# Gated DeltaNet projections: convolution taps and SiLU traced later, decays a head ahead, last blocks reordered

## The chip, the cores and the metric

The kernel runs on one core of a Trainium2 chip. The metric is device time in microseconds of one execution. The engines named below are PE (TensorE), DVE (VectorE), ACT (ScalarE), POOL (GpSimd) and SP (SyncE, which here issues DMAs). Each takes its own instructions strictly in the order in which the compiled program holds them.

## The reference

A trunk of two layers over two groups of tokens, one of 1024 and one of 256, which the kernel handles as T = 1280 tokens. Layer 0 is a neighbourhood attention, layer 1 a bidirectional gated DeltaNet with 8 heads (keys of 128, values of 256, chunks of 64). The change is in layer 1:

```python
proj = h @ w_in
qkv = jax.nn.silu(_centred_depthwise_conv(proj[..., :o1], conv_w))   # 5 taps along the tokens
z = proj[..., o1:o2].reshape(b, t, GDN_HEADS, GDN_DV)
...
decay = jnp.where(tril, jnp.exp(jnp.where(tril, diff, 0.0)), 0.0)
a_kk = jnp.where(tril_strict, jnp.einsum('bhncd,bhnsd->bhncs', k_beta, k) * decay, 0.0)
lhs = jnp.eye(c, dtype=jnp.float32) + a_kk
w = lax.linalg.triangular_solve(lhs, k_beta * jnp.exp(g)[..., None], ...)
u = lax.linalg.triangular_solve(lhs, v * beta[..., None], ...)
...                                     # a scan over chunks, forward and backward
o = _rmsnorm(o, norm_w) * jax.nn.silu(z)
return o.reshape(b, t, GDN_VW) @ w_out
```

## The kernel before, in words

**Stages.** Layer 0 fills the first 750 us. `gdn_proj` (about 760 to 1600) makes everything that the scan of layer 1 needs: for each of 8 heads four blocks of 128 channels of q, k and v, and two blocks of z. Then `prep(..., alone=True)` prepares head 0, the scan of the heads runs (1633 to 2000), and the output projection ends the program.

**A block** is 128 channels times 1280 tokens, in three column pieces (512, 512, 256). For each piece PE runs 24 float matmuls (three products of high and low parts over eight slices of the width, line L1203) into a PSUM bank `mm`, which has three buffers. For q, k and v ACT copies the piece into a `raw` tile with borders for the convolution (L516). Then come the convolution's centre tap `acc` on ACT (L519), four further taps on DVE (L521, 128x1282 each), SiLU on ACT (`th`, L524), and a DMA to `qkv_spill` in DRAM (L525, L526). Channel `ch` of head `h` is 0 for q, 1 for k, 2 and 3 for v; the loop takes (0,1), then for each head 0, 2, 3 and the next head's 1. A z block takes tanh on ACT (L546) and a product on DVE (L549).

**The inversion.** As soon as a head's k is there, `invert` turns it into the inverse of the triangular matrices, all ten pairs of chunks at once:
- decays E: a matmul into a PSUM tile `t` (L584; `t` has three buffers), four additions on DVE (L587), Exp on ACT (L590), a DMA to `e_spill`, and the sum B of both directions on POOL (L604);
- pk = k.k on PE, also into `t` (L608), its diagonal (`junk`, L612) and B (L616) on DVE;
- D (L623), the transpose N (L632), X (L633), then **the sweep**: 30 steps of two DVE instructions, each depending on the last (L638, L640), and two transposes (L644, L645);
- copies of X on ACT (L653, L654) and of parts of W on POOL; then a wait of 34000 columns;
- four small groups of matmuls: L666, then Z on ACT (L669), L673, then DVE and ACT (L675 to L681), L686, Z (L689), L694, W (L696), and a DMA to `w_spill` (L697).

**What sets the order.** A `Side` object holds generators. While the block matmuls are traced, `side.tick(columns)` adds up their columns, and a generator whose due time is reached is traced up to its next `yield n`, after which it is due n columns later (times a pace). A block has 30,720 columns. The framework's scheduler then orders each engine's instructions from this trace; `keep_in_program_order` pins an instruction behind what was traced before it on its engine. In before, the taps and SiLU are traced at once after their block, and `invert` starts 26000 to 50000 columns behind its k block.

**The hand-over.** `factors` (L795 to L820) makes reciprocal square roots on DVE, with one small DMA. `prep` asks on SP for kT, qT, the decays Al, qe, vT and W (L840 to L859), all from DRAM, and its three groups of matmuls lead to the scan's first matmul (L967).

## Time and profile before

| | |
|---|---|
| median of 3 runs | 2265.09 us (2259.45 to 2268.21) |
| the profiled execution | 2260.98 us; span on the core 2259.2 us |
| mean granted clock of PE | 0.977 of full speed |
| DVE, ACT, POOL busy | 1509.4, 1127.4, 571.9 us |

The median lies 4 us above the profiled execution, whose durations are used throughout. A row of the profile has an engine, a line of the kernel, an operation and `out<-in` by tile names, then the shape and `xN` for N instructions; a number in square brackets is the idle time before it, with the engine and instruction that ended it. In a timeline the first number is the start in us from the span's start and the second the duration. PE's matmuls are pipelined: the distance between two starts is what one costs.

### The profile page before, as it was taken

What the parts mean: (1) busy time and instruction counts of PE and PEld (TensorE: products, weight loads), DVE (VectorE), ACT (ScalarE), POOL (GpSimd) and SP (SyncE); (2) the same over time, 40 slices, a digit from 0 to 9 for tenths busy, and PEclk for the clock granted to TensorE, in tenths of its full rate; (3) what the DMA queues carried; (4) which work ended last, traced back from release to release, by engine and by line L of the source; (5) the groups of instructions that cost most, each with busy time, mean ns of one, the idle gap of its engine ahead of it and who ended that gap; (6) DMA issues with size and microseconds to landing.
All of it is one profiled execution on the core that took longest, in us unless ns stands there. A gap on an engine that the chain in (4) does not pass through costs nothing.

```text
span 2259.2 us, 34060 instructions
## 1 busy us (share of the span) xinstructions
PE 2170.7 (96%) x12502; PEld 1885.4 (83%) x12502; DVE 1509.4 (67%) x3370; ACT 1127.4 (50%) x2299; POOL 571.9 (25%) x634
## 2 busy tenths in 40 slices
PE   8999999999989998999999999999799999999998
PEld 7789989989878877878888888888688888877887
DVE  5577777776763867858586776868466666676444
ACT  6455545555573454443444444454356666654233
POOL 2100100110231422212232222223176666600000
PEclk9999999999999998999999999999699999999999
DMA  5434343533555343535435353452575565567322
GB/s 180 111 74 117 81 117 74 124 93 99 154 156 170 97 114 103 148 93 133 135 101 162 91 146 100 145 143 78 182 206 166 167 186 179 149 217 234 109 96 85
DMA packets 148457, 300.10 MB, mean 133 GB/s; under 512 B 44977, under 2 KB 67633, under 8 KB 147265
## 3 DMA queue, kind: packets, MB, share of 16 engines
q1 hardware_dynamic: 126784, 232.89, 32.7%
q0 software_dynamic: 12096, 44.05, 11.1%
q10 hardware_dynamic: 9408, 20.98, 3.0%
q8 instruction: 99, 1.62, 0.3%
q14 instruction: 70, 0.57, 0.1%
HBM read 211.92 MB, written 75.45 MB: 127 GB/s over the span
## 4 chain that ended last, share of the span: by engine, by line
PE 36%; DVE 17%; ACT 4%; DMA 3%; issue 2%; POOL 1%; SPq 0%; DVEq 0%; ACTq 0%; POOLq 0%
PE mm L1203 17%; DVE acc L521 5%; DVE tmp L638 4%; DVE X L640 4%; PE k L967 3%; PE o L939 2%; PE u L939 2%; PE o L980 2%; PE k L958 2%; DMA e_spill<-E 1%; PE t L893 1%; PE m L1049 1%; DVE N L644 1%; PE m L673 1%; DMA yt<-y_spill 1%
## 5 line engine op out<-in xcount | busy, mean ns | idle before, releaser
L1203 PE MATMUL mm<-xh,wl 128*128 128x512 f32 (+1 forms) x1920 | 701.8, 366 | 3.9 <-DMA wl<-w_o 3.0
L1203 PE MATMUL mm<-xl,wh 128*128 128x512 f32 (+1 forms) x1920 | 702.7, 366 | 0.3 <-DVE xl L352 0.2
L1203 PE MATMUL mm<-xh,wh 128*128 128x512 f32 (+1 forms) x1920 | 701.3, 365 | 1.6 <-DVE t L189 0.7
L1203 PEld LDWEIGHTS mm<-xh,wl 128*128 128x128 f32 x1920 | 367.8, 192 | 47.2 <-DMA wl<-w_o 3.4
L1203 PEld LDWEIGHTS mm<-xh,wh 128*128 128x128 f32 x1920 | 367.9, 192 | 46.1 <-POOL xh L351 1.1
L1203 PEld LDWEIGHTS mm<-xl,wh 128*128 128x128 f32 x1920 | 367.5, 191 | 44.1 <-DVE xl L352 0.4
L521 DVE SCALAR_TENSOR_TENSOR acc<-raw,cw,acc 128x1282 f32<-128x1282 f32 x128 | 201.3, 1573 | 84.6 <-ACT acc L519 82.9
L1153 POOL CAST wh<-wraw 128x1024 fp32r<-128x1024 f32 x32 | 33.7, 1054 | 497.6 <-PE mm L1203 441.3
L1155 ACT ACTIVATE wh<-wraw 128x1024 fp32r<-128x1024 f32 x92 | 96.9, 1055 | 99.5 <-PE mm L1203 75.1
L1203 PE MATMUL mm<-yh,wh 128*128 128x512 f32 (+1 forms) x384 | 137.5, 359 | 2.4 <-ACT yh L1077 2.4
L1203 PE MATMUL mm<-yh,wl 128*128 128x512 f32 (+1 forms) x384 | 137.0, 358 | 1.2 <-DVE wl L1157 1.2
L1203 PE MATMUL mm<-yl,wh 128*128 128x512 f32 (+1 forms) x384 | 137.7, 360 | 0.3 <-DVE yl L1078 0.3
L971 DVE TENSOR_TENSOR vl<-k,vh 128x256 fp32r<-128x256 f32 x160 | 66.9, 422 | 69.9 <-ACT vh L970 65.4
L247 ACT ACTIVATE ph<-pt 128x512 fp32r<-128x512 f32 (+2 forms) x144 | 67.5, 478 | 76.0 <-PE pt L243 64.5
L248 DVE TENSOR_TENSOR pl<-pt,ph 128x512 fp32r<-128x512 f32 (+2 forms) x144 | 75.1, 538 | 37.7 <-ACT ph L247 36.1
L524 ACT ACTIVATE th<-acc 128x1282 f32<-128x1282 f32 x32 | 40.9, 1278 | 113.3 <-DVE acc L521 113.3
L1159 ACT ACTIVATE wl<-wraw 128x1024 fp32r<-128x1024 f32 x84 | 88.8, 1057 | 16.2 <-DMA wraw<-w_qk 8.1
L516 ACT ACTIVATE raw<-mm 128x512 f32<-128x512 f32 (+1 forms) x96 | 49.7, 521 | 94.2 <-PE mm L1203 93.0
L221 ACT ACTIVATE P<-P,mx 128x384 f32<-128x384 f32 (+1 forms) x128 | 75.0, 586 | 39.6 <-DVE mx L220 38.3
L1219 PE MATMUL mm<-wh,xl 128*128 128x256 f32 x320 | 92.4, 289 | 0.3 <-POOL xl L65 0.3
L1219 PE MATMUL mm<-wh,xh 128*128 128x256 f32 x320 | 92.3, 290 | 0.0
L1219 PE MATMUL mm<-wl,xh 128*128 128x256 f32 x320 | 92.1, 288 | 0.0
(315 smaller groups left out, 4871.8 us busy)
## 6 DMA issues: line engine op xcount, KB each, us to landing
wraw<-w_qkv SPq DMA_DIRECT2D x32, 512.0 KB, 3.9
qkv_spill<-th SPq DMA_DIRECT2D x32, 512.0 KB, 2.6
wraw<-w_go SPq DMA_DIRECT2D x32, 512.0 KB, 3.4
wl<-w_qkv POOLq DMA_DIRECT2D x30, 512.0 KB, 7.4
Al<-e_spill SPq DMA_DIRECT2D x8, 1280.0 KB, 6.8
qe<-eg_spill SPq DMA_DIRECT2D x16, 640.0 KB, 7.9
wraw<-w_qk SPq DMA_DIRECT2D x16, 512.0 KB, 4.0
wl<-w_qk POOLq DMA_DIRECT2D x16, 512.0 KB, 8.9
```

Of the source, the lines that this page charges most:

```text
L221: nc.scalar.activation(Pv, Pv, AF.Exp, scale=-1.0, bias=mx[:, 0:1], accum_out=mx[:, 1:2])
L247: nc.scalar.activation(view(ph), view(pt), AF.Copy)
L248: nc.vector.tensor_sub(view(pl), view(pt), view(ph))
L521: nc.vector.scalar_tensor_tensor(acc, r[:, i:i + m], cw[:, f, i:i + 1], acc, op0=OP.mult, op1=OP.add)
L638: nc.vector.tensor_mul(tv, N[:, 0:c, c:c + 1].to_broadcast([128, c, n]), X[:, c:c + 1, c + 1:32].to_broadcast([128, c, n]))
L640: nc.vector.tensor_add(X[:, 0:c, c + 1:32], X[:, 0:c, c + 1:32], tv)
L939: self.tc.nc.tensor.matmul(ps, w[x], v[y], start=(first and i == 0), stop=(i == 2))
L967: nc.tensor.matmul(pw, W[:, d, cs[d]], Y[d], start=True, stop=True)
L1155: nc.scalar.activation(wh, raw, AF.Copy)
L1159: nc.scalar.activation(wl, raw, AF.Copy, scale=-1.0)
L1203: nc.tensor.matmul(ps, w[:, k, :], x[k][b], start=(k == 0 and i == 0), stop=(k == KD - 1 and i == 2))
L1219: nc.tensor.matmul(ps, x[k][b][:, cc], w[:, k % 4, :], start=(k == 0 and i == 0), stop=(k == KD - 1 and i == 2))
```

## The change

- The taps and SiLU of a block become a generator `conv`. The taps are traced 8000 columns after the block and the first is pinned on DVE; SiLU is traced 14000 columns later for k and 20000 for the others, and pinned on ACT. `invert` is added from there, 4000 columns later.
- `raw` has two buffers in place of three, B two in place of one.
- The decays leave `invert` and become a generator `decays`. Head 0's follow the gates; head h+1's are added 4000 columns behind the sweep of head h. `invert` waits until they exist.
- `factors` moves from behind `gdn_proj` to the same point of head 7; its pool `cp` opens earlier.
- A z block's product and DMA become a generator `gated`, 3000 columns later, pinned on DVE.
- The last blocks: k of head 7 now comes ahead of the last v block of head 6. One z block follows head 7's k, and one the loop.
- In `prep`, when it runs alone, the vT loads come ahead of the others, the first two before Al.

Of the instructions only the table loads of ACT change in number, 34 to 48, and POOL's memsets by three.

```diff
@@ -466,11 +466,12 @@
         ap = st.enter_context(pool(tc, "gp", 2, "right"))
         pp = st.enter_context(banks(tc, "gpi", 2, "right"))
         side = a["side"] = Side()
-        side.add(gates(tc, a, ap, pmm, pp, XH, XL))
+        Bs = {}
+        side.add(chained(gates(tc, a, ap, pmm, pp, XH, XL), decays(tc, a, ap, pp, 0, Bs)))
         side.tick(0)
         cw = ap.tile([128, 32, 5], F32, name="cw", bufs=1)
         nc.sync.dma_start(cw, a["conv_w"])
-        raw = [ap.tile([128, T + 6], F32, name=f"raw{i}", bufs=1) for i in range(3)]
+        raw = [ap.tile([128, T + 6], F32, name=f"raw{i}", bufs=1) for i in range(2)]
         for r in raw:
             nc.gpsimd.memset(r[:, 0:2], 0.0)
             nc.gpsimd.memset(r[:, NP + 2:NP + 4], 0.0)
@@ -500,10 +501,32 @@
                 h, i = next(zs)
                 gate_z(tc, a, pmm, XH, XL, h, side, (i,))
 
-        for h, ch in [(0, 1)] + [(h + (ch == 1), ch) for h in range(8) for ch in (0, 2, 3, 1)][:-1]:
+        def conv(f, r):
+
+            h, ch = divmod(f, 4)
+            m = T + 2
+            acc = ap.tile([128, T + 2], F32, name="acc")
+            nc.scalar.activation(acc, r[:, 2:2 + m], AF.Copy, scale=cw[:, f, 2:3])
+            yield 8000
+            for i in (0, 1, 3, 4):
+                tap = nc.vector.scalar_tensor_tensor(acc, r[:, i:i + m], cw[:, f, i:i + 1], acc,
+                                                     op0=OP.mult, op1=OP.add)
+                if i == 0:
+                    tc.keep_in_program_order(tap)
+            yield 14000 if ch == 1 else 20000
+            th = ap.tile([128, T + 2], F32, name="th")
+            tc.keep_in_program_order(nc.scalar.activation(th, acc, AF.Silu))
+            nc.sync.dma_start(a["qkv_dram"][f, :, :NP], th[:, :NP])
+            nc.sync.dma_start(a["qkv_dram"][f, :, NP:], th[:, NP + 2:])
+            if ch == 1:
+                side.add(invert(tc, a, ap, pp, h, th, D, W, WT, Z, Bs), 4000, 0.85 if h == 7 else 0.95)
+
+        order = [(0, 1)] + [(h + (ch == 1), ch) for h in range(8) for ch in (0, 2, 3, 1)][:-1]
+        order[27:29] = order[28:26:-1]
+        for h, ch in order:
             f = 4 * h + ch
             wh, wl = a["first"].pop(0) if a["first"] else load_w(tc, a, a["w_qkv"][f])
-            r = raw[n_c % 3]
+            r = raw[n_c % 2]
             n_c += 1
             for b in sorted(range(3), key=lambda b: (f, b) not in a["begun"]):
                 t0, n = BLK[b]
@@ -514,23 +537,11 @@
                     proj(nc, ps, wh, wl, XH, XL, b, side)
                 o = 2 if t0 < NP else 4
                 nc.scalar.activation(r[:, t0 + o:t0 + o + n], ps, AF.Copy)
-            m = T + 2
-            acc = ap.tile([128, T + 2], F32, name="acc")
-            nc.scalar.activation(acc, r[:, 2:2 + m], AF.Copy, scale=cw[:, f, 2:3])
-            for i in (0, 1, 3, 4):
-                nc.vector.scalar_tensor_tensor(acc, r[:, i:i + m], cw[:, f, i:i + 1], acc,
-                                               op0=OP.mult, op1=OP.add)
-            th = ap.tile([128, T + 2], F32, name="th")
-            nc.scalar.activation(th, acc, AF.Silu)
-            nc.sync.dma_start(a["qkv_dram"][f, :, :NP], th[:, :NP])
-            nc.sync.dma_start(a["qkv_dram"][f, :, NP:], th[:, NP + 2:])
+            side.add(conv(f, r), 0)
+            side.tick(0)
             if ch == 1:
-                delay = {0: 32000, 1: 50000, 2: 37000}.get(h, 26000)
-                side.add(invert(tc, a, ap, pp, h, th, D, W, WT, Z), delay, 0.87 if h == 7 else 0.95)
-                if h != 1:
-                    gate_blocks(2 if h else 1)
-            elif (h, ch) == (1, 0):
-                gate_blocks(2)
+                gate_blocks(1 if h in (0, 7) else 2)
+        gate_blocks(1)
         side.drain()
 
 
@@ -538,6 +549,12 @@
 
     nc = tc.nc
     ws = [load_w(tc, a, a["w_z"][2 * h + i]) for i in halves]
+
+    def gated(u, z, ps, t0, n):
+        tc.keep_in_program_order(nc.vector.scalar_tensor_tensor(z, z, 1.0, ps, op0=OP.add, op1=OP.mult))
+        nc.sync.dma_start(a["z_dram"][u, :, t0:t0 + n], z)
+        yield 0
+
     for i, (wh, wl) in zip(halves, ws):
         for b, (t0, n) in enumerate(BLK):
             ps = pmm.tile([128, 512], F32, name="mm")[:, :n]
@@ -546,8 +563,12 @@
             tanh = nc.scalar.activation(z, ps, AF.Tanh, scale=0.5)
             if h == 7 and i:
                 tc.keep_in_program_order(tanh)
-            nc.vector.scalar_tensor_tensor(z, z, 1.0, ps, op0=OP.add, op1=OP.mult)
-            nc.sync.dma_start(a["z_dram"][2 * h + i, :, t0:t0 + n], z)
+            side.add(gated(2 * h + i, z, ps, t0, n), 3000)
+
+
+def chained(*gens):
+    for g in gens:
+        yield from g
 
 
 def alternate(*gens):
@@ -590,18 +611,30 @@
     nc.scalar.activation(E, E, AF.Exp)
 
 
-def invert(tc, a, ap, pp, h, kT, D, W, WT, Z):
+def decays(tc, a, ap, pp, h, Bs):
 
     nc = tc.nc
-    B = ap.tile([128, NB, 128], F32, name="B", bufs=1)
+    B = ap.tile([128, NB, 128], F32, name="B", bufs=2)
     for c0 in range(0, NB, 4):
         n = min(4, NB - c0)
         E = ap.tile([128, 2, 4, 128], F32, name="E", bufs=1)[:, :, :n]
         for d in range(2):
             decay(nc, a, ap, pp, h, d, c0, n, E[:, d], 3)
-            yield 2000
+            yield 3500
         nc.sync.dma_start(a["e_dram"][h, :, :, c0:c0 + n], E)
         nc.gpsimd.tensor_add(B[:, c0:c0 + n], E[:, 0], E[:, 1])
+    Bs[h] = B
+
+
+def invert(tc, a, ap, pp, h, kT, D, W, WT, Z, Bs):
+
+
+    nc = tc.nc
+    while h not in Bs:
+        yield 400
+    B = Bs.pop(h)
+    for c0 in range(0, NB, 4):
+        n = min(4, NB - c0)
         pk = pp.tile([128, 4, 128], F32, name="t", bufs=3)
         for c in range(n):
             k = kT[:, tok(c0 + c)]
@@ -660,6 +693,10 @@
         nc.gpsimd.tensor_copy(W[sl[i], 0, :, q], diag(i, 1 - lo))
         nc.gpsimd.tensor_copy(W[sl[i], 1, :, q], diag(i, lo))
         yield 0
+    if h < 7:
+        a["side"].add(decays(tc, a, ap, pp, h + 1, Bs), 4000)
+    else:
+        factors(tc, a)
     yield 34000
     zt = pp.tile([128, NB, 32], F32, name="m", bufs=2)
     for c in range(NB):
@@ -800,10 +837,10 @@
         nc.vector.scalar_tensor_tensor(y, t, 1.5, y, op0=OP.add, op1=OP.mult)
 
 
-def factors(tc, a, cp):
+def factors(tc, a):
 
     nc = tc.nc
-    ss = a["ss"]
+    ss, cp = a["ss"], a["cp"]
     nw = cp.tile([128, 2], F32, name="nw")
     nc.sync.dma_start(nw, a["norm_w"])
     nc.vector.tensor_scalar(nw, nw, 0.5, None, op0=OP.mult)
@@ -844,19 +881,29 @@
     AH, AL = (ap.tile([128, 2, NB, 128], F32R, name=f"A{p}") for p in "hl")
     qe = ap.tile([128, 2, T], F32, name="qe")
     sq = ap.tile([128, NB], F32, name="sq")
+    vT = []
+
+    def rows(*bs):
+        for b in bs:
+            t0, n = BLK[b]
+            for i in range(2):
+                t = tp.tile([128, n], F32, name=f"vT{b}{i}")
+                nc.sync.dma_start(t, a["qkv_dram"][4 * h + 2 + i, :, t0:t0 + n])
+                vT.append(t)
+
+    if alone:
+        rows(0)
     nc.sync.dma_start(AL.bitcast(F32), a["e_dram"][h])
+    if alone:
+        rows(1, 2)
     for d in range(2):
         nc.sync.dma_start(qe[:, d], a["eg_dram"][8 * d + h].partition_broadcast(128))
-    vT = []
-    for b, (t0, n) in enumerate(BLK):
-        for i in range(2):
-            t = tp.tile([128, n], F32, name=f"vT{b}{i}")
-            nc.sync.dma_start(t, a["qkv_dram"][4 * h + 2 + i, :, t0:t0 + n])
-            vT.append(t)
+    if not alone:
+        rows(0, 1, 2)
     lo, hi = slice(0, 64), slice(64, 128)
     for d, (own, other) in enumerate(((lo, hi), (hi, lo))):
-        for i, rows, cols in ((0, other, other), (1, own, own), (2, own, other)):
-            nc.sync.dma_start(W[rows, d, :, cols], a["w_dram"][h, rows, i])
+        for i, rows_, cols in ((0, other, other), (1, own, own), (2, own, other)):
+            nc.sync.dma_start(W[rows_, d, :, cols], a["w_dram"][h, rows_, i])
     X[:] = kT, V, K, qe, (AH, AL), W, sq
     yield 28000 if alone else 6000
     for c0 in range(0, NB, 4):
@@ -1302,16 +1349,15 @@
     XH, XL, pmm, mm_ctx = layer0(ctx, tc, a, h1)
     left.callback(mm_ctx.close)
     a["gc"] = right.enter_context(pool(tc, "gc", 1, "right"))
+    a["cp"] = right.enter_context(pool(tc, "cp", 1, "right"))
     a["ss"] = a["gc"].tile([128, 8, NB], F32, name="ss")
     a["nrk"] = a["gc"].tile([128, 8, NB], F32, name="nrk")
     a["zp"] = left.enter_context(pool(tc, "zp", 2))
     gdn_proj(tc, a, pmm, XH, XL)
-    cp = right.enter_context(pool(tc, "cp", 1, "right"))
     p_m = right.enter_context(banks(tc, "p_m", 1, "right"))
     p_0 = left.enter_context(banks(tc, "p_0", 4))
     tp = even.enter_context(pool(tc, "prep", 1, "right"))
     ap = [even.enter_context(pool(tc, "even", 1, "right"))]
-    factors(tc, a, cp)
     W = [whole(nc, ap[0])]
     X = [[], []]
     side = Side()
```

What it does to the order, at three places. First DVE behind the sweep of a late head (the sweep's two transposes write N and D; `acc` rows are taps; E from `t` are decays). Before:

```order
L644 STREAM_TRANSPOSE N_12827<-X_12551 128x32x32
L645 STREAM_TRANSPOSE D_8873<-X_12551 128x32x32
L521 SCALAR_TENSOR_TENSOR acc_12887<-raw0_8847,cw_8845,acc_12887 128x1282 x4
L521 SCALAR_TENSOR_TENSOR acc_12993<-raw1_8848,cw_8845,acc_12993 128x1282 x3
L675 STREAM_TRANSPOSE WT_8875<-m_13031 32x10x32
```

After:

```order
L677 STREAM_TRANSPOSE N_12790<-X_12519 128x32x32
L678 STREAM_TRANSPOSE D_8872<-X_12519 128x32x32
L512 SCALAR_TENSOR_TENSOR acc_12756<-raw1_8851,cw_8848,acc_12756 128x1282 x2
L608 SCALAR_TENSOR_TENSOR E_12846<-t_12847,lbG_8977,mask_8858 128x128
L512 SCALAR_TENSOR_TENSOR acc_12756<-raw1_8851,cw_8848,acc_12756 128x1282
L608 SCALAR_TENSOR_TENSOR E_12846<-t_12847,lbG_8977,mask_8858 128x128
L512 SCALAR_TENSOR_TENSOR acc_12756<-raw1_8851,cw_8848,acc_12756 128x1282
L608 SCALAR_TENSOR_TENSOR E_12846<-t_12847,lbG_8977,mask_8858 128x128 x2
L608 SCALAR_TENSOR_TENSOR E_12846<-t_12861,lbG_8977,mask_8858 128x128 x4
```

The next head's decays now stand behind the sweep, mixed with one block's taps; no taps are inside a late head's sweep any more.

Second, DVE inside the sweep of head 7. Before, one block's four taps stand there:

```order
L638 TENSOR_TENSOR tmp_15293<-N_15119,X_15120 128x220
L521 SCALAR_TENSOR_TENSOR acc_15310<-raw2_8849,cw_8845,acc_15310 128x1282
L640 TENSOR_TENSOR X_15120<-X_15120,tmp_15293 128x11x20
L521 SCALAR_TENSOR_TENSOR acc_15310<-raw2_8849,cw_8845,acc_15310 128x1282
L638 TENSOR_TENSOR tmp_15303<-N_15119,X_15120 128x210
L521 SCALAR_TENSOR_TENSOR acc_15310<-raw2_8849,cw_8845,acc_15310 128x1282
L640 TENSOR_TENSOR X_15120<-X_15120,tmp_15303 128x10x21
L521 SCALAR_TENSOR_TENSOR acc_15310<-raw2_8849,cw_8845,acc_15310 128x1282
```

After, those of two blocks (the first row here is already the second tap of the first block):

```order
L512 SCALAR_TENSOR_TENSOR acc_15102<-raw0_8850,cw_8848,acc_15102 128x1282
L673 TENSOR_TENSOR X_14994<-X_14994,tmp_15148 128x10x21
L512 SCALAR_TENSOR_TENSOR acc_15102<-raw0_8850,cw_8848,acc_15102 128x1282
L671 TENSOR_TENSOR tmp_15154<-N_14993,X_14994 128x198
L512 SCALAR_TENSOR_TENSOR acc_15102<-raw0_8850,cw_8848,acc_15102 128x1282
L673 TENSOR_TENSOR X_14994<-X_14994,tmp_15154 128x9x22
L512 SCALAR_TENSOR_TENSOR acc_15296<-raw1_8851,cw_8848,acc_15296 128x1282
L671 TENSOR_TENSOR tmp_15160<-N_14993,X_14994 128x184
L512 SCALAR_TENSOR_TENSOR acc_15296<-raw1_8851,cw_8848,acc_15296 128x1282
L673 TENSOR_TENSOR X_14994<-X_14994,tmp_15160 128x8x23
```

Eight taps now stand between the sweep's steps in place of four. Third, SP at the hand-over. Before:

```order
L525 DMA qkv_spill<-th 128x1024
L526 DMA qkv_spill<-th 128x256
L550 DMA z_spill<-z 128x512
L808 DMA nw<-norm_w 128x2
L840 DMA kT<-qkv_spill 128x1280
L841 DMA qT<-qkv_spill 128x1280
L847 DMA Al<-e_spill 128x2560
L849 DMA qe<-eg_spill 128x1280 x2
L854 DMA vT_15688<-qkv_spill 128x512
```

After:

```order
L519 DMA qkv_spill<-th 128x1024
L520 DMA qkv_spill<-th 128x256
L555 DMA z_spill<-z 128x256
L877 DMA kT<-qkv_spill 128x1280
L878 DMA qT<-qkv_spill 128x1280
L891 DMA vT_15681<-qkv_spill 128x512
L891 DMA vT_15683<-qkv_spill 128x512
L896 DMA Al<-e_spill 128x2560
L891 DMA vT_15686<-qkv_spill 128x512
```

The last `th` now goes out a z block ahead of the end of PE's blocks, and the preparation's loads follow the end of the z block before the last.

## Prediction

> **What bounds the kernel now.** I read the page first, then the waits of PE, then PE's timeline at those waits, then the granted clock beside them.
>
> ```profile
> PE 2170.7 (96%) x12502; PEld 1885.4 (83%) x12502; DVE 1509.4 (67%) x3370; ACT 1127.4 (50%) x2299; POOL 571.9 (25%) x634
> PEclk9999999999999998999999999999699999999999
> ```
>
> PE is busy 96% of the span, so the change can win only PE's idle time and the slices below full clock. The waits of PE over the input projections and the hand-over to the scan (760 to 1640 us; columns: total, times, longest):
>
> ```profile
> PE m L666 <- ACT X L653: 14.8, 3, 8.6
> PE m L673 <- ACT Z L669: 12.2, 6, 4.6
> PE t L608 <- DVE E L587: 1.1, 1, 1.1
> ```
>
> The chain of a head's inversion is what PE waits for: X (behind DVE's sweep) and Z (behind ACT). Three of these waits are long:
>
> ```profile
> 893.27 4.45 PE L666 MATMUL m<-X,B 128*128 128x32 f32 x20 [8.58 <-ACT X L653]
> 989.72 0.63 PE L673 MATMUL m<-X,Z 128*128 128x32 f32 x2 [4.57 <-ACT Z L669]
> 1081.47 0.59 PE L666 MATMUL m<-X,B 128*128 128x32 f32 x2 [4.49 <-ACT X L653]
> ```
>
> They are heads 0, 1 and 2. The other waits for Z are short, (12.2 - 4.57) / 5 = 1.5 us each. The granted clock in the 10.2 us behind a wait (the value after POOL's):
>
> ```profile
> 893.30:903.50 10.20, 10.20 (x55) 9.99 (x56) 0.00 (x0) 5.96 (x10) 2.77 (x7) 0.64 0.17 66
> 989.80:1000.00 10.20, 10.20 (x35) 8.95 (x36) 3.45 (x3) 3.42 (x4) 2.02 (x2) 0.52 0.58 142
> 1081.60:1091.80 10.20, 10.20 (x35) 8.89 (x36) 6.21 (x4) 4.98 (x9) 1.28 (x3) 0.50 0.47 104
> 1184.40:1194.60 10.20, 10.20 (x59) 8.95 (x60) 6.77 (x8) 4.27 (x6) 2.03 (x2) 1.00 0.62 166
> 1281.60:1291.80 10.20, 10.20 (x37) 8.76 (x38) 6.60 (x8) 2.87 (x3) 2.02 (x2) 0.56 0.48 103
> 1383.60:1393.80 10.20, 10.20 (x41) 8.79 (x42) 6.85 (x8) 2.90 (x3) 2.03 (x2) 0.67 0.46 103
> ```
>
> The wait costs twice: 8.6 us is followed by clock 0.64 (10.2 x 0.36 = 3.7 us of work lost), 4.5 us by 0.50 to 0.52 (about 5.0 us lost). A 1.5 us wait was followed by full clock in head 3 (1184), by 0.56 and 0.67 in heads 4 and 5 (4.5 and 3.4 us lost); head 6 I count with head 3.
>
> So before loses: head 0, 8.6 + 3.7 = 12.3; head 1, 4.6 + 4.9 = 9.5; head 2, 4.5 + 5.1 = 9.6; heads 3 to 6, 4 x 1.5 + 7.9 = 13.9; head 7, about 3.1 (below).
>
> **What the change removes.** Why Z is late in every late head shows on ACT:
>
> ```profile
> 1278.51 0.41 ACT L669 ACTIVATE Z<-m 32x320 f32<-32x320 f32 x1
> 1278.83 1.35 ACT L519 ACTIVATE acc<-raw,cw 128x1282 f32<-128x1282 f32 x1
> 1280.20 1.31 ACT L669 ACTIVATE Z<-m 32x320 f32<-32x320 f32 x3
> ```
>
> A convolution's centre tap, 1.35 us, stands between the first Z copy and the other three. In the changed order the four copies stand together in the late heads, and more matmuls lie ahead of each step, so the 1.5 us at Z should go. The decays also leave the path from k to the sweep.
>
> **What it adds: a wait at the decays.** The next head's decays now come right after a sweep. PE's "t" tiles have three buffers, so PE's fourth decay matmul waits until DVE has read the first tile; on DVE those reads stand behind the sweep, two transposes and four pinned taps. I time both engines from the first k.k matmul (pk) of a late head. DVE, from head 5's records:
>
> ```profile
> 1327.10 0.29 DVE L612 CUSTOM_DVE_ANT_0 junk<-t,ident 128x128 f32<-128x128 f32 x1
> 1330.20 1.12 DVE L587 SCALAR_TENSOR_TENSOR E<-t,lbG,mask 128x128 f32<-128x128 f32 x4
> 1333.74 2.05 DVE L623 STREAM_TRANSPOSE D<-B 32x320 f32<-32x320 f32 x4
> 1335.89 2.17 DVE L632 STREAM_TRANSPOSE N<-D 128x1024 f32<-128x1024 f32 x1
> 1355.09 1.54 DVE L521 SCALAR_TENSOR_TENSOR acc<-raw,cw,acc 128x1282 f32<-128x1282 f32 x1
> 1361.80 0.35 DVE L640 TENSOR_TENSOR X<-X,tmp 128x198 f32<-128x198 f32 x1
> 1367.18 2.21 DVE L644 STREAM_TRANSPOSE N<-X 128x1024 f32<-128x1024 f32 x1
> 1369.27 2.06 DVE L645 STREAM_TRANSPOSE D<-X 128x1024 f32<-128x1024 f32 x1
> ...
> L549 DVE SCALAR_TENSOR_TENSOR z<-z,mm 128x512 f32<-128x512 f32 (+1 forms) x18 | 10.6, 587 | 15.9 <-ACT z L546 15.9
> ```
>
> Up to N: 0.6 for pk, ten junk steps at 0.33 (its own 0.29 and a read-out), reciprocals 0.6, ten B (as long as an E read, 1.12 / 4 = 0.28), two z products (1.0), the four transposes 2.1: 10.2 us. From N to the end of the second transpose the trace has 1371.33 - 1335.89 = 35.4 us with four taps inside; from the first tap to the record at 1361.80 are 6.7 us for four taps and three short sweep steps of about 0.37, so a tap inside a sweep costs 1.4 and the sweep without them 29.8. The change puts three z products there (one stood there before), about +1.3: 31.1 us. Then four taps and the four reads of the first decay tile, about 4 x 1.54 + 1.1 = 7.3. Sum 10.2 + 31.1 + 7.3 = 48.6 us.
>
> PE, in the changed order, has between the same two points 144 projection matmuls of 512 columns, 86 of 256, ten pk and three decays:
>
> ```profile
> 1100.13 0.39 PE L1203 MATMUL mm<-xh,wl 128*128 128x512 f32 x1
> 1100.36 0.40 PE L1203 MATMUL mm<-xh,wh 128*128 128x512 f32 x1
> 1329.23 0.71 PE L608 MATMUL t<-th 128*128 128x128 f32 x4
> 1598.34 0.28 PE L1203 MATMUL mm<-xh,wh 128*128 128x256 f32 x1
> 1598.46 0.28 PE L1203 MATMUL mm<-xl,wh 128*128 128x256 f32 x1
> ```
>
> 144 x 0.227 + 86 x 0.12 + 1.5 + 0.7 = 45.2 us. PE waits 48.6 - 45.2 = 3.4 us, in heads 2 to 6. Bounds: 1 us if DVE is at N earlier, 5 us if the z products don't overlap. No row shows the clock after 3.4 us; 4.5 us always lost 5, 1.5 us in two of four. I take the loss, being nearer in effect to the first: 3.4 + 4.9 = 8.3 a head.
>
> Heads 3 to 6: 33.2 against 13.9, **+19**. Head 2: 8.3 against 9.6, **-1**. Head 1's decays start early in its sweep, where the same ring waits 2 to 3 us; its other waits go: 2.5 against 9.5, **-7**.
>
> **Heads 0 and 7.** Here eight taps stand inside the sweep, and the X matmul right behind it. Head 7: PE has 173 x 0.227 + 72 x 0.12 + 2 = 49.9 us from pk to L703. DVE has 10.2 to N, 29.4 without z, 8 x 1.4 = 11.2 for taps, and the square-root steps of factors, now there (about 18 of the kind below, 4.3): 55.1, and from there to the matmul 3.2 (1569.76 to 1572.93):
>
> ```profile
> 1595.00 0.24 DVE L800 SCALAR_TENSOR_TENSOR r<-rt,r 128x80 f32<-128x80 f32 x1
> 1567.68 2.08 DVE L645 STREAM_TRANSPOSE D<-X 128x1024 f32<-128x1024 f32 x1
> 1572.93 0.38 PE L666 MATMUL m<-X,B 128*128 128x32 f32 x2 [1.74 <-ACT X L653]
> ```
>
> 58.3 - 49.9 = 8.4 us, and 3.7 of clock, as after head 0's 8.6. Before it was 1.74 and about 1.4 at Z: **+9**. Head 0 by the same count waits 6.6 us at L703. Behind it L710, L723, L731 and head 1's pk stand within four thousand columns (under 2 us of PE), while pk waits for a Silu behind four taps, 6.2 us, and its table load: about 8 us more. 6.6 + 8 + twice 3.7 of clock = 22.0 against 12.3, **+10**.
>
> **The hand-over to the scan.**
>
> ```profile
> 1596.72 0.53 SPq L840 DMA_DIRECT2D kT<-qkv_spill  x1
> 1600.74 0.28 PE L1203 MATMUL mm<-xh,wl 128*128 128x256 f32 x1
> 1603.94 2.05 PE L868 MATMUL t<-qT,kT 128*128 128x128 f32 x8 [2.92 <-DMA qT<-qkv_spill]
> 1618.23 1.86 PE L880 MATMUL t<-ones,q 128*128 128x1 f32 x8 [2.61 <-ACT q L877]
> 1632.87 2.04 PE L967 MATMUL k<-V,W 128*128 128x256 f32 x4 [2.04 <-POOL W L828]
> ```
>
> From the last z matmul to the scan's first are 32 us. SP asks for kT 4 us ahead of that matmul, behind the last Silu. Now the last convolution stands a z block earlier and kT some 23 thousand columns, 10 us, ahead of the end, so preparation's first group (1603.94 to 1618.23) runs largely beside the z block; groups two and three (14.6 us) stay, and E still waits for Al: 32 to about 21, **-11**, between -4 (loads wait for a buffer) and -15. Taking factors out gives nothing of its own: DVE idles there for the loads.
>
> At nothing: two raw buffers (PE's next block is 13.8 us behind, and the taps begin 8000 columns, 3.6 us, after a block), B's second buffer, nw's earlier load. The fourteen added ACT table loads:
>
> ```profile
> L524 ACT ACT_TABLE_LOAD x9 | 11.5, 1283 | 0.2
> ```
>
> 14 x 1.283 = 18 us on an engine half idle. Two of them stand, in each late head, between the last decays and the Z copies. PE has some 17 thousand columns (7.6 us) and L703 there; ACT has the two loads (2.6), a Silu, two exponentials and the four copies (1.7), and stays ahead by two to three us. [...]
>
> **Sum:** 19 - 1 - 7 + 9 + 10 - 11 = +19 us on the profiled 2260.98: 2280. The median of the runs, 2265.09, lies 4 above that execution; half of it added, 2282.
>
> **Rivals.**
> - The clock holds. If 3.4 us lets it stand, five losses of 4.9 go: 2282 - 24 = 2258, no change. For it speaks head 3's row, against it heads 4 and 5. [...]
> - Faster: the decays find DVE ahead. If DVE reaches N some 2 us earlier than I count, or the short steps fill gaps between taps, the ring's wait falls to 1 us and below and the clock stands: 2282 - 5 x 8 = 2242. It decides from a ring wait under about 1.5 us. For it: DVE is busy 67% of the span only; against: this chain is serial, and DVE has no gap in it.
> - The hand-over gains nothing, because kT's buffer comes free late: 2293. For it: kT's issue waits for PE in the new order; against: PE passes that point 10 us before the end.
>
> **Chances.** The forecast 0.50 (its own range 2268 to 2300), the clock holds 0.22, DVE ahead 0.20, no gain at the hand-over 0.08. The range takes 2238 to 2302. Within 0.5% (2254 to 2276, about what a measurement can tell from no change) falls the clock's case and a little of the first: 0.25. Slower 0.51, faster 0.24.
>
> **What would show it.** In the profile after: waits "PE t L605 <- DVE E" of about 3.4 us in five heads, clock near 0.5 behind them; L710's waits gone from late heads; L703's of 6 to 9 us in heads 0 and 7 only; about 21 us from the last z matmul to L1014. Wrong would be a ring wait under 1.5 us, or a quiet head 0.

## The result, and the profile after

| | before | after |
|---|---|---|
| median (4 runs each) | 2263.84 us (2259.45 to 2268.21) | 2250.47 us (2249.23 to 2251.55) |
| the profiled execution's span | 2259.2 us | 2249.7 us |

The ratio is 0.9941, with a 95% interval of 0.992 to 0.9962: the change makes the kernel 0.6% faster. The prediction, 2282 with slower as the likeliest side, was wrong in its sign. Its range held the time.

The page of after, PE's busy time and its granted clock in 40 slices:

```profile
PE 2166.0 (96%) x12502; PEld 1881.3 (84%) x12502; DVE 1509.2 (67%) x3370; ACT 1146.6 (51%) x2313; POOL 585.1 (26%) x631
PEclk9999999999999999899999999999899999999999
```

Where the clock row of before had a 6 (the 29th slice, the hand-over), after has an 8. The waits of PE from the start of head 1's own blocks to that of head 7's (1000 to 1500 us), two rows of before and the one of after (columns: total, times, longest):

```profile
PE m L673 <- ACT Z L669: 6.2, 4, 1.7
PE m L666 <- ACT X L653: 4.5, 1, 4.5
```

```profile
PE t L605 <- DVE E L608: 16.6, 5, 3.3
```

The five waits at the decays are there, 3.3 us each where the prediction had 3.4, and the waits at Z are gone. So PE waits 16.6 us in place of 10.7. Yet the stretch is hardly longer. The rest is clock. The windows view of after, around the wait in the stretch of heads 1 and 2 (four rows) and the last of the five (three); columns are the window, its length, PE's busy time, the granted clock, and DMA:

```profile
1057.60:1061.02 3.42, 2.03 (x17) 1.00 0.00 0
1061.02:1064.43 3.41, 1.49 (x8) 1.00 0.00 0
1064.43:1067.84 3.41, 3.41 (x10) 0.50 0.40 154
1067.84:1071.26 3.42, 3.42 (x17) 1.00 0.71 175
1460.38:1463.79 3.41, 1.70 (x15) 1.00 0.00 0
1463.79:1467.21 3.42, 1.81 (x9) 1.00 0.00 0
1467.21:1470.62 3.41, 3.41 (x17) 1.00 0.40 154
```

The windows are cut at multiples of 3.413 us from the first drop. I call an unbroken stretch at half clock a spell. But for the last of each profile, the spells of before and after are 3.41, 6.83, 10.24, 13.65 or 34.13 us long, whole multiples of 3.413. All twelve spells of after begin within 3 ns of such a grid, and those of every other profile here within 4 ns of their own. In four of the five places the wait of 3.3 us falls on two windows. In the first place 1.92 us of it lie in the second window, and the next one runs at half clock. In the last place they split into 1.71 and 1.61 us, and nothing drops. In the four places that dropped, the half-clock window that projection matmuls filled (PE busy for 3.12 to 3.42 us of it) was followed by full clock.

That gives the time between 1000 and 1500 us a simple account: waits plus half of the half-clock spells. Before: 10.7 + 27.3 / 2 = 24.4 us. After: 16.6 + 17.1 / 2 = 25.1. The starts of the blocks in PE's timeline agree: from the 15th block to head 7's first, 468.5 us before and 470.0 after, 1.5 us more where the account has 0.7.

The gain stands at the end. From head 7's first block to the scan's first matmul took 134.4 us before (1498.5 to 1632.9) and 121.2 after (1501.5 to 1622.7). PE's waits in that stretch, before and then after ("issue" is a wait for nothing that the profile shows):

```profile
PE t L880 <- ACT q L877: 6.0, 3, 2.6
PE t L868 <- DMA qT<-qkv_spill: 2.9, 1, 2.9
PE t L893 <- ACT V L894: 2.1, 2, 1.6
PE k L967 <- POOL W L828: 2.0, 1, 2.0
PE m L666 <- ACT X L653: 1.7, 1, 1.7
PE t L893 <- DMA vT<-qkv_spill: 1.4, 1, 1.4
PE m L673 <- ACT Z L669: 1.4, 1, 1.4
```

```profile
PE m L703 <- issue: 4.1, 1, 4.1
PE t L940 <- ACT V L941: 3.4, 3, 2.6
PE t L927 <- ACT q L924: 3.4, 1, 3.4
```

17.5 us of waits became 10.9, which is 6.6 of the 13.2 us. Before, the clock was at half from 1603.73 to the scan, 29.1 us. After, it was so in two spells, 10.24 us in head 7 and 5.3 us of the one ahead of the scan. PE waited inside these spells too: it was busy for 17.3 of the 29.1 us and for 10.6 of the 15.5. So half clock gives (17.3 - 10.6) / 2 = 3.4 us more, and the last 3 us, also less busy time of PE, are not traced. Part of the cause shows on PE's timeline; the preparation now runs beside the last z block, at full clock (it was granted from 1566.19 to 1617.39 us):

```profile
1600.86 1.05 PE L915 MATMUL t<-qT,kT 128*128 128x128 f32 x8
1601.67 0.48 PE L1250 MATMUL mm<-xl,wh 128*128 128x512 f32 x1
1605.00 0.83 PE L915 MATMUL t<-qT,kT 128*128 128x128 f32 x6
...
1609.81 0.28 PE L1250 MATMUL mm<-xh,wl 128*128 128x256 f32 x1
1619.66 1.01 PE L927 MATMUL t<-ones,q 128*128 128x1 f32 x4 [3.35 <-ACT q L924]
1622.67 1.06 PE L1014 MATMUL k<-V,W 128*128 128x256 f32 x2
```

The first of its three groups (L915 x8) and the start of the second (L915 x6) stand before the last z matmul (1609.81). From there to the scan are 12.9 us, 32.1 before.

### The profile page after: what moved, and what is told of

The parts are those of the page before. It is cut to its first block, busy times and chain, and to the rows that moved or that the text cites. A ratio compares the mean times of both kernels' runs of the same rounds, so it can differ in the third digit from the quotient of the medians.

```text
span 2249.7 us, 34012 instructions
## 1 busy us (share of the span) xinstructions
PE 2166.0 (96%) x12502; PEld 1881.3 (84%) x12502; DVE 1509.2 (67%) x3370; ACT 1146.6 (51%) x2313; POOL 585.1 (26%) x631
## 4 chain that ended last, share of the span: by engine, by line
PE 70%; DVE 17%; ACT 5%; DMA 4%; issue 3%; POOL 1%; SPq 0%; ACTq 0%; DVEq 0%; POOLq 0%
PE mm L1250 42%; PE mm L1266 4%; DVE tmp L671 3%; DVE X L673 3%; PE k L1014 3%; PE o L986 2%; PE k L1005 2%; PE O L263 2%; PE o L1027 2%; PE u L986 2%; DVE acc L512 2%; PE pt L243 2%; DMA yt<-y_spill 1%; PE t L940 1%; PE S L286 1%
## 5 line engine op out<-in xcount | busy, mean ns | idle before, releaser
L539 ACT ACTIVATE raw<-mm 128x512 f32<-128x512 f32 (+1 forms) x96 | 49.9, 522 | 101.9 <-PE mm L1250 96.1
L608 DVE SCALAR_TENSOR_TENSOR E<-t,lbG,mask 128x128 f32<-128x128 f32 x160 | 46.9, 342 | 79.7 <-DMA e_spill<-E 78.8
L1017 ACT ACTIVATE vh<-k 128x256 fp32r<-128x256 f32 x160 | 60.6, 380 | 62.5 <-PE k L1014 59.3
```

## The experiments

Two theories were tested. **A**: the clock is lost by the 3.413 us windows of this grid, so what counts is how much of one window is idle and what PE does in the windows behind. **B**, the prediction's: a wait of some 3 us or more costs about 4.9 us of clock. Medians are each beside the kernel before on the same chip (2265 to 2268 us). The changed kernel had 2263.84 us beside it, so between kernels the ratios to before are the safer comparison. The waits, spells and stretches are read from one profile of each kernel.

**e1: the decays later still.** In `invert`:

```diff
-        a["side"].add(decays(tc, a, ap, pp, h + 1, Bs), 4000)
+        a["side"].add(decays(tc, a, ap, pp, h + 1, Bs), 14000)
```

> The changed kernel with the next head's decays added 14000 columns behind the sweep in place of 4000; nothing else. If the five waits of 3.3 us at the fourth decay matmul come from DVE's sweep, transposes and taps ahead of the first decay tile, they vanish (PE comes there 10000 columns, 4.5 us, later), and with them the half-clock windows behind them: 5 x 3.3 + 8 = about 25 us less than the changed kernel, near 2226 us. Rival: the wait moves on to Z (ACT's table loads and exponentials then stand closer to the Z copies), and less than 10 us is gained.

2267.94 us, 1.0009 of before (0.9995 to 1.0023). The wait did not go: it moved to the sixth decay matmul, 3.5 to 3.6 us in each of five heads, since the kernel gives E one buffer and the sixth stands behind the whole chain of the others (in the second of the five, DVE itself waits 6.0 us for the DMA out of E, `DVE E L608 <- DMA e_spill<-E`). That wait is 7% longer than in after, but the spells behind it were 10.24, 13.65, 10.24, 13.65 and 13.65 us, 61.4 in sum against 17.1. The sixth decay matmul stands right ahead of the solve's first small matmuls (128x32 out), which are issued one between two large ones. The second of the five, as windows:

```profile
1167.07:1170.48 3.41, 3.41 (x17) 1.00 0.49 192
1170.48:1173.89 3.41, 0.37 (x2) 1.00 0.56 195
1173.89:1177.31 3.42, 2.94 (x11) 0.50 0.87 204
1177.31:1180.72 3.41, 3.41 (x14) 0.50 0.33 65
1180.72:1184.13 3.41, 3.41 (x13) 0.50 0.00 0
1184.13:1187.55 3.42, 3.42 (x16) 0.50 0.00 0
1187.55:1190.96 3.41, 3.41 (x28) 1.00 0.39 154
```

PE is busy throughout from 1177, and still three more windows run at half clock. B can't give that: nearly the same wait, another spell.

**e2: a longer wait, large matmuls behind it.** Twelve products on a scratch tile, pinned on DVE behind the sweep in heads 2 to 6:

```diff
+    if 2 <= h <= 6:
+        pad = ap.tile([128, 128], F32, name="junk", bufs=1)
+        for _ in range(12):
+            tc.keep_in_program_order(nc.vector.scalar_tensor_tensor(pad, a["ident"], 1.0, a["ident"],
+                                                                   op0=OP.mult, op1=OP.mult))
```

> The changed kernel with twelve useless DVE products (128x128) pinned behind the sweep in heads 2 to 6, so that the wait at the decays grows from 3.3 to about 6 us; projection matmuls follow it as before. Theory A (the clock drops for a window in which PE idled more than about half, and comes back after one full window of large matmuls): one or two half-clock windows of 3.4 us behind each wait. Theory B (the length of the wait sets the loss: 4.5 us and more cost three windows, as in the kernel before): three windows, 10.2 us, behind each.

2277.71 us (one run). The wait grew to 5.6 us in all five heads and the spell behind each to 6.83: one whole window idle, 1.65 us of the next, then one full window. So a wait 2 us longer than e1's has a shorter spell, 6.83 against 10.24 to 13.65. A new wait for `raw` came besides (8.5 us in all), a cost of the longer wait that none had named.

**e3: the small matmuls right behind the wait.** In `invert`, heads 2 to 6:

```diff
-    yield 34000
+    yield 15500 if 2 <= h <= 6 else 34000
```

> The changed kernel with the wait of 34000 columns ahead of L703 cut to 15500 in heads 2 to 6, so that the ten small 128x32 matmuls of L703, one between two projection matmuls, follow right behind the wait at the decays; the wait's length stays near 3.3 us. Theory A with its second half (small matmuls hold the clock down): two or three half-clock windows behind each wait in place of one. Theory B (length alone): one, as in the changed kernel.

2260.56 us (one run). Waits of 3.2 us as in after; spells 6.83, 10.24, 6.83, 10.24 and 6.83 us, 41.0 in sum against 17.1.

**e4: the scan's loads in the old order.** `rows(0)` and `rows(1, 2)` ahead of the others taken out, all vT loads behind Al and qe:

> The changed kernel with the preparation's loads in the order of before (Al, qe, then all vT); blocks and all else as changed. If the new order of loads carries a part of the hand-over's gain, the scan starts 4 to 8 us later than in the changed kernel; if the earlier last convolution (the order of blocks) carries it all, within 2 us.

2255.44 us, 0.9955 of before (0.9938 to 0.9971). From the start of the last block to the scan's first matmul are 34.7 us in place of 30.9, so the order of the loads makes some 3.8 us of the 13.2, just under the 4 to 8 expected. From head 7's first block on PE waits 12.2 us in place of 10.9; the rest goes with half clock, which begins 8.7 us earlier ahead of the scan (1608.69 in place of 1617.39).

**e5: the decays spread out**, so that neither the fourth nor the sixth stands early:

```diff
-            yield 3500
+            yield 5500 if h else 3500
-        a["side"].add(decays(tc, a, ap, pp, h + 1, Bs), 4000)
+        a["side"].add(decays(tc, a, ap, pp, h + 1, Bs), 9000)
```

> The changed kernel with the decays added 9000 instead of 4000 columns behind the sweep, and 5500 instead of 3500 columns between two of them (heads 1 to 7), so that in the order both the fourth and the sixth decay matmul of a head stand later behind VectorE's queue, and the sixth no longer stands right ahead of the solve's first small matmul. Theory that the clock loses by windows (a window of 3.41 us with over about 1.7 us idle halves the next one, and small matmuls behind it keep it halved): the five waits of 3.3 us shrink under 1.5 us each or go, no half-clock spell is left in heads 2 to 6, and the time falls by 5 x 3.3 us of waits and some 8 us of clock, to 2222 to 2232. Rival, that the wait only moves on to another decay matmul, as it did with 14000 columns: five waits of 3 to 3.6 us at the sixth matmul, with spells of 6.8 to 13.7 us where the solve's small matmuls follow: 2250 to 2268.

2222.08 us, 0.9791 of before (0.9766 to 0.9817), as theory A had it. Of PE's waits from 874 to 1500 us only head 0's are left:

```profile
PE m L703 <- ACT X L686: 5.5, 1, 5.5
PE m L723 <- DVE WT L713: 1.9, 1, 1.9
PE m L723 <- ACT Z L726: 1.0, 1, 1.0
```

And the windows view over heads 1 to 6 in one row:

```profile
1000.00:1500.00 500.00, 500.00 (x2814) 1.00 0.48 134
```

PE is busy all of the 500 us, at full clock. A late head takes 95.4 us in place of 100.4. Two numbers that set the order gave 28 us beyond the changed kernel by the medians (some 34 by the ratios to before), twice what the change itself gave.

**e6: head 0's solve later.** Its 34000 columns behind the sweep made 50000, only there:

> The changed kernel with head 0's solve begun 50000 instead of 34000 columns behind its sweep (the other heads as they are). In the changed kernel the stretch from head 1's first block to the seventh block after it is 14.4 us longer than before the change, with waits of 4.6 us at the solve's first matmul, 0.5 and 1.7 us at its later steps and 2.6 us at a gate block, and half-clock spells of 10.2 and 13.7 us. If the wait for the solve's input is its cause: the 4.6 us wait goes, and with it the first spell, the stretch is 6 to 10 us shorter, the time 2240 to 2245. If the packing of the solve's last steps is its cause, they are packed as closely here: the stretch stays within 3 us of what it was, with the half-clock spells standing later: 2248 to 2253.

2246.2 us (one run). Neither expectation fits. The wait for X went, but 4.0 us moved to the sixth decay matmul ahead of it and 2.8 us to the third step; the stretch is 3.7 us shorter.

**e7: the last blocks in the old order** (the swap in `order` taken out, both z blocks behind head 7's k):

> The changed kernel with the last blocks in the order that they had before the change (head 7's k block behind head 6's last value block, and both gate blocks right behind it); all else as changed. The prediction held that this order costs head 7 about 9 us by an earlier solve and gives some of the hand-over back. If the order of the blocks makes the shorter hand-over (51.1 us from the last-but-one block's start to the scan before, 30.9 us after, of which the order of the scan's loads made 3.8 us): the hand-over is 10 to 16 us longer than in the changed kernel, head 7's stretch up to 10 us shorter, and the time 2250 to 2260. If the rest of the tail made it (the factors ahead of the end of the projections): the hand-over stays under 35 us, head 7 gains, and the time is 2238 to 2246.

2258.45 us, 0.9954 of before (0.9935 to 0.9973). From the start of the last block to the scan 41.2 us, 10.3 longer than in after (the expectation's 51.1 and 30.9 are counted from the last block too, and not from the one before it); head 7's wait fell to 0.4 us. From head 7's first block to the scan the net is 126.9 against 121.2: the order of the blocks is worth some 5.7 us there. That is the first of the two expectations. The whole times of e4 and e7, 0.9955 and 0.9954 against 0.9941, don't tell these kernels from the changed one, so both sizes rest on one profile each.

**e8: the kernel before, with the small matmuls packed.** One line taken out behind each of two matmuls, so that ten come in one go:

```diff
         nc.tensor.matmul(zt[:, c], B32[:, c], M[:, c], start=True, stop=True)
-        yield 0
...
         nc.tensor.matmul(w[:, c], Z[:, c], M[:, NB + c], start=True, stop=True)
-        yield 0
```

> The kernel before the change with the ten small matmuls (128x32 out) of the solve's first step, and those of its second, each issued in one go instead of one between two large matmuls of the projections; nothing else. In the kernel before they follow a wait of about 1.6 us in heads 2 to 6, and spells of half clock of 3.4 to 10.2 us stand there. If small matmuls mixed among large ones hold the clock at half: the spells behind the first step in heads 1 to 6 shrink to 3.4 us or go, the sum of spells in that part falls by 15 to 25 us, the time by 7 to 12 us, to 2252 to 2258. If a wait's length alone sets the spell, or the wait itself grows since the group comes as one: the spells stay as they are, within 5 us in sum, and the time within 5 us of the kernel before.

2245.54 us, 0.9901 of before (0.988 to 0.9922): more than the whole change. But it doesn't isolate the clock, as two things moved: with the first ten done sooner, Z is ready sooner, and PE's wait for it fell too, from 6.2 us in four waits of 1.5 to 1.7 us to 1.9 us in four of at most 0.5. Spells between 1000 and 1500 fell from 27.3 to 17.1 us, 10 us and not the 15 to 25 expected. In head 2, where the wait of 4.7 us stayed, the spell stayed 10.24 us.

**e9: room for head 7 as well.** e5 with

```diff
-                side.add(invert(tc, a, ap, pp, h, th, D, W, WT, Z, Bs), 4000, 0.85 if h == 7 else 0.95)
+                side.add(invert(tc, a, ap, pp, h, th, D, W, WT, Z, Bs), 4000, 0.95)
-    yield 34000
+    yield 44000 if h == 7 else 34000
```

> The version with the decays spread out (9000 and 5500 columns, time 2222.1), and head 7's solve later: pace 0.95 instead of 0.85, and its first small matmul 44000 instead of 34000 columns behind the sweep, which puts it some 10 thousand columns (4.4 us of PE) later and its last three steps 13 to 31 thousand columns apart instead of 2 to 7. There PE waited 4.7 us for the solve's input, with a half-clock spell of 10.2 us behind it. Theory of the windows: the wait falls under 1 us, no window has 1.9 us idle, the spell goes, head 7 up to the scan is 7 to 10 us shorter: 2211 to 2216. Rival: the solve's end now stands at the hand-over and the scan waits for its buffers, so that what is won in head 7 is lost behind it: 2219 to 2226.

**2214.79 us, 0.9779 of before (0.9759 to 0.98)**, the fastest version, 36 us under the changed kernel. Head 7's wait of 4.7 us and its spell are gone. From head 7's first block to the scan are 117.5 us, e5 had 123.0; the hand-over gave 5.0 us of it back (35.9 against 30.9), as the rival had it in part.

```profile
PE 2147.9 (97%) x12502; PEld 1868.7 (84%) x12502; DVE 1511.1 (68%) x3370; ACT 1148.4 (52%) x2315; POOL 598.7 (27%) x631
```

PE's busy time is 18 us under that of after with the same 12502 matmuls, since fewer of them ran at half clock: the mean granted clock was 0.987 in place of 0.980.

**e10: head 1's decays behind head 0's solve** (e9, and 45000 columns in place of 9000 there):

> The same, and in head 0 the decays of head 1 put 45000 instead of 9000 columns behind the sweep, so that they stand behind the solve's first two steps rather than ahead, and the next steps stand 15 to 30 thousand columns apart. Theory: head 0's wait of 5.5 us at the solve's first matmul is VectorE's and ScalarE's work on these decays ahead of the solve's input; without it the wait falls to 2 us or less and the spells of 13.7 and 6.8 us shrink to 3.4 to 7 in sum; 6 to 12 us faster than the version before: 2200 to 2208. Rival: the input is late for another cause (the taps and gate products in head 0), the wait stays over 4 us, and the late decays make waits of their own of some 3 us: within 4 us of the version before, or slower.

2219.71 us, 0.9795 of before (0.9766 to 0.9824), not faster than e9. The rival was right: head 0's wait for X stayed at 5.2 us, and the late decays made a wait of their own, 2.7 us. What makes X late in head 0 stays open.

**e11: without the three ties in program order** (first tap, SiLU, gate product):

> The changed kernel without the three ties in program order (first tap, Silu, gate product); all else as changed. In its order the taps still stand behind the sweep, one ahead of the decay reads, and one gate product less inside the sweep. If the ties are what keeps the taps out of the sweep and thereby makes the change's gain: waits at the solve's steps come back and the time is over 2260. If the delays in columns do that and the ties only hold the decay reads behind four taps: the five waits of 3.3 us at the fourth decay matmul shrink to 1 to 3 us, and the time is 2235 to 2250.

2248.86 us, 0.9929 of before (0.9907 to 0.9951), no different from the changed kernel. The five waits are 3.0 to 3.1 us, so the expected fall to 1 to 3 us hardly came. The equal time is a net: the decays behind the sweeps of heads 0 and 1 have new waits of 4.5 and 4.4 us, and from head 7's first block to the scan it is 113.9 us in place of 121.2. The delays in columns keep the order in heads 2 to 6; what the ties do at the two ends is not taken apart.

**e12: factors behind the projections again:**

> The changed kernel with the norm factors issued behind the projections as before the change, instead of in head 7's solve; all else as changed. From head 7's first block to the scan took 134.4 us before and 121.2 us after; the order of the loads made 3.8 us of the 13.2 and the order of the blocks 5.6. The prediction gave this part nothing at the hand-over and some 4.3 us of VectorE ahead of head 7's solve. If so: head 7's wait of 4.1 us at the solve's first matmul falls under 1 us with its spell, the hand-over is at most 2 us longer, and the time 2240 to 2247. If the factors' place makes the missing 3.8 us: the hand-over is 3 to 6 us longer, and the time 2248 to 2255.

2254.06 us (2243.8 to 2259.26), 0.9941 of before (0.9923 to 0.9959), as the changed kernel. Both parts of the expectation missed. Head 7's wait stays (4.1 in after), and the hand-over from the last block's start is 30.9 us in both:

```profile
PE m L701 <- issue: 4.2, 1, 4.2
```

But this did not do what it was meant to. The call moved in the program, and in DVE's order the steps of `factors` (rt, nrk) still stand among the first steps of head 7's sweep (L671, L673), as in after:

```profile
1521.02 0.21 DVE L671 TENSOR_TENSOR tmp<-N,X 128x30 f32<-128x30 f32 x1
1521.14 0.19 DVE L852 TENSOR_SCALAR nrk<-nrk 128x80 f32<-128x80 f32 x1
1521.26 0.22 DVE L673 TENSOR_TENSOR X<-X,tmp 128x30 f32<-128x30 f32 x1
1521.38 0.23 DVE L833 TENSOR_TENSOR rt<-r 128x80 f32<-128x80 f32 x1
```

What moved is one block's four taps, out of head 7's sweep to behind it, and PE came to the solve's first matmul earlier too. So this run says nothing of the place of `factors`. From head 7's first block to the scan its profile takes 124.9 us, 3.7 more than after; the spell behind the wait is 17.07 us in place of 10.24.

**e13: e1 with the small matmuls packed,** the test that e8 was not, since here the wait stands ahead of them:

> The version with the decays 14000 columns behind the sweep (2267.9), whose wait of 3.5 us stands right ahead of the solve's first ten small matmuls, with these ten and the second step's ten each issued in one go instead of one between two large matmuls. The wait ahead of them can't change by this. There the half-clock spells behind the five waits were 10.24, 13.65, 10.24, 13.65 and 13.65 us. Theory that a half-clock window with six or more small matmuls never lets the clock return: packed, the ten fill one window and large matmuls the next, the spells fall to 3.4 to 7 us, 25 to 40 us less in sum, and the time by 12 to 20 us, to 2248 to 2256. Rival, that the wait and its place alone set the spell: spells as they were, 2262 to 2270.

The waits stayed at 3.56 to 3.58 us. All five spells became 6.83 us, 34.1 in sum against 61.4:

```profile
1167.25:1170.66 3.41, 0.52 (x5) 1.00 0.77 266
1170.66:1174.08 3.42, 3.42 (x18) 0.50 0.97 156
1174.08:1177.49 3.41, 3.41 (x10) 0.50 0.03 5
1177.49:1180.90 3.41, 3.41 (x25) 1.00 0.00 0
```

Here one half-clock window takes the small matmuls, the next holds large ones only, and the clock is back at 1177.49. The time missed: 2264.84, 0.9984 of before (0.997 to 0.9998), 3 us under e1 (some 6 by the ratios to before) and not 12 to 20. From head 3's first block to head 7's (1100.1 to 1511.0, in e1 1102.1 to 1521.3) it is 8.3 us shorter, but head 0's stretch (the 7th block's start to the 13th's) became 7 us longer, with new waits of 2.5 and 1.2 us at head 1's decays. Its profiled execution took 2258.31 us and e1's 2275.55, each at an end of its range, so these stretches say less than the medians.

**e14: e9 with the small matmuls packed:**

> The fastest version so far (decays spread, head 7's solve later, 2214.8) with the same packing. It has no half-clock spell in heads 1 to 7 left, and one of 13.65 us in head 0 behind a wait of 5.3 us. Theory: that spell shrinks to 10.2 us or less, 2 to 4 us; nothing to win elsewhere: 2210 to 2214. Rival: ten small matmuls in one go leave a whole window nearly without work of the kind that counts, and make new spells in heads 1 to 7 where there is no wait at all: 2218 to 2230.

2225.4 us, 0.9805 of before (0.9778 to 0.9833), 11 us above e9 by the medians and some 6 by the ratios, whose intervals overlap. In the profiles most of it is in head 0 again (126.0 us against 118.6). The rival has its case too, in one head of six:

```profile
1356.28:1359.69 3.41, 2.89 (x25) 1.00 0.44 87
1359.69:1363.11 3.42, 3.42 (x18) 0.50 0.00 0
```

Here a window with 0.52 us of idle time and twenty small matmuls was followed by half clock.

**The windows counted.** I cut the time from 1000 to 1500 us of before, after and the fourteen experiments into the windows of each profile's own grid. Of windows at full clock without small matmuls and with over 1 us idle, the 34 with 1.91 us or more halved the next one, and the 23 with 1.88 or less did not. Of half-clock windows without small matmuls the 41 with up to 0.45 us idle gave the clock back and the 14 with 0.63 or more did not. Of half-clock windows with six or more small matmuls, none of 27 gave it back, 23 of them without a gap of as much as 0.15 us; with one to five small ones, nine of 14 did. That is theory A, and B is out.

One measure covers these four counts. I added up the columns of the matmuls in each of the 2,328 windows, each matmul's spread over its own time: 0.227 us for 512 columns at full clock, the distance between their starts in before and after, and twice that at half (the distance there is 0.427 us, and a count with it moves no window of before or after by more than 30 columns). All 89 windows with fewer than 2,800 columns were followed by half clock and all 2,216 with more than 3,180 by full clock, whichever clock they had themselves; the 23 between are mixed. In before and after a window at full clock holds up to 7,710 columns and one at half some 4,100, and before's half-clock windows with eight small matmuls among the large ones hold 2,304. So in these profiles the two limits of idle time come to nearly one number of columns, and small matmuls need not act by themselves: they leave fewer columns in a window. This is counted and not tested by a run of its own. From 760 to 1000 and 1500 to 1640 us, where other kinds of matmul stand, the mixed band is wider (1,660 to 3,350).

## Why the prediction was wrong

Point by point, predicted and measured:

| term | predicted | measured |
|---|---|---|
| waits at the decays, heads 2 to 6 | 5 x 3.4 = 17.0 | 16.6 |
| clock lost behind them | 5 x 4.9 = 24.5 | 17.1 / 2 = 8.5 |
| what before lost in heads 2 to 6 | 23.5 | 24.4 |
| heads 0 and 1 together | +3 | -0.3 |
| head 7 and the hand-over together | +9 - 11 = -2 | -13.2 |

The right column doesn't add up to the 9.5 us between the two profiles: by the starts of the blocks, heads 2 to 6 are 1.5 us longer and not 0.7, the blocks ahead of head 0's stretch 1.8 and the time from the scan on 0.7.

- **The step that failed** is "I take the loss, being nearer in effect to the first", the 4.9 us of clock for a wait of 3.4 us: 16 us of the 28 by which the sum was off. Its rows were true, but they measured something else. In before, small matmuls stood one between two large ones behind those waits, and the clock stayed down for two to four windows (6.83 to 13.65 us). In the changed order large ones stand there. The prediction sized the loss by the wait's length and never looked at what PE does behind it, though the windows that it quoted from before had it: PE busy all of 1081.60 to 1091.80, and clock 0.50.
- **The wait of 3.4 us** came out at 3.3 in part by luck. From the first k.k matmul of a late head to the wait's end are 46.8 us and not 48.6, as DVE is at N after 8.2 and not 10.2 (the terms written for it add up to 10.4); PE without its wait takes 43.5 and not 45.2, with 73 matmuls of 256 columns in place of 86. Both sides were about 1.8 us too long.
- **Heads 4 and 5 of before**, which dropped after 1.5 us and seemed to speak against a clock that holds after 3.4 us, fit the count: their waits of 1.55 and 1.51 us stood with eight small matmuls each in one window, which held 2,161 and 1,920 columns.
- **The rival "the clock holds"** was the nearer one in kind. It was no all or nothing: the clock held in one head of five and lost one or two windows in four.
- **"DVE ahead"** was wrong for after (3.3 us, not 1), although DVE did reach N 2.0 us earlier than counted, since PE was earlier too. Its price, 8 us a head, was too high: e5, where the decays do find DVE ahead, saves 5.0 us a head (95.4 against 100.4).
- **The hand-over** was the second mis-sized term; with head 7 it was off by 11 us. From the last z matmul to the scan are 12.9 us where the prediction had about 21, so 8 of the 11 us are there; the other 3 are in head 7 (6.1 us longer up to that matmul, not 9). The prediction counted which groups come beside the z block, and not that all of that stretch ran at half clock in before (29.1 us). The early kT was right: SP asks for it at 1593.25, 16.6 us ahead of the last z matmul. Of the 13.2 us the block order makes some 5.7 (e7) and the order of the loads 3.8 (e4), if the two add; the rest is not traced to an edit, and what the place of `factors` does to it stays open.
- **Head 7's wait** was 4.1 us, not 8.4. From the first k.k matmul to the solve's first, DVE's chain and the copy of X take 55.8 us and not 58.3, and PE without its wait 51.7 and not 49.9. The 4.3 us charged for `factors` were too much. Its steps stand between the sweep's first ones: from N to the 32nd of them head 7 takes 15.9 us, a late head with three z products (about 0.65 us each) 16.8. That leaves some 1.4 us for `factors`, an estimate that has 0.3 us ahead of N in it.
- **Heads 0 and 1** are given together because the solve's last steps and head 1's products moved across the border between them. L703 waits 4.6 us in head 0 (6.6 predicted), and the 8 us at pk did not come.
- **Right**: the waits at Z go from late heads; the fourteen added table loads, 1.283 us each in after as in before, cost PE nothing that shows: from 760 to 1640 us no wait at L710 is listed.

## What to carry to other kernels

Where PE's clock drops, cut the time on the grid of the drops and look at two things: how much of one window a wait takes, and what stands behind it. In these profiles full-clock windows without small matmuls halved the next from 1.91 us idle of their 3.413 on and did not up to 1.88; half-clock windows with six or more small matmuls were followed by another in all 27 cases. Spread or shorten a wait until no window is that idle, and keep small matmuls away from the windows behind one; the columns counted in a window sum up both (half clock followed below 2,800, full clock above 3,180). An engine's wait that is 3 us long and repeated is worth moving by hand: two numbers in the order (e5) gave 28 us, more than the whole change with its 13.

Small matmuls are not simply better packed or better spread. Packed, they freed the clock behind a wait (e13) and halved it with a wait of only 0.5 us (e14); what separates the two in the count is the columns left in a window.

## What the hardware showed that I had not expected

- PE stayed at half clock without a wait: 23 half-clock windows without a gap of 0.15 us, with six or more small matmuls among the large ones, were each followed by another at half clock. PE counts as busy there (3.41 of 3.41 us in before's window at 1084.90); by columns, eight small ones leave that window at 2,304 of some 4,100.
- The same wait of 3.3 us cost 0, 1.7 or 3.4 us of clock in after (spells of none, 3.41 and 6.83 us), by where it fell on the grid.
- The same order of work falls differently on the grid from run to run: e4's profile has two spells between 1000 and 1500 us, after's and e12's four, with the same five waits. The runs of e12 spread over 15 us, and the clock goes with them: four at 0.984 or 0.985 take 2243.8 to 2250.1 us, six at 0.979 or 0.98 take 2252.1 to 2259.3.
